# Seven block products in place of eight for 28 pairs of row tiles in the down projection

## The chip, the cores and the metric

The kernel runs on one core of one Trainium2 chip. The metric is device time in microseconds (us) of one execution; lower is better. Three runs of the kernel before gave 2377.18, 2375.62 and 2376.84 us, median 2376.84 us. A profile is one more execution, taken by the hardware profiler, with a time of its own.

Engines are named as the profile names them: PE (TensorE's matmuls), PEld (its weight loads), DVE (VectorE), ACT (ScalarE), POOL (GpSimd), SP (SyncE, which issues most of the transfers).

## The reference

Two layers, each a mixer and a gated MLP, on x of 256 rows by 2048 columns, all float32. The change concerns the last product of the MLP:

```python
def conv_ffn(h, w_gate, w_up, conv_w, conv_b, w_down):
    ...
    return (jax.nn.silu(conv) * (h @ w_up)) @ w_down

def reference(x, ...):
    for l in range(DEPTH):
        h = rms_norm(x, ln1_g[l])
        x = x + hybrid_mixer(h, w_in[l], ret_norm_g[l], q_norm_g[l], k_norm_g[l], w_out[l])
        h = rms_norm(x, ln2_g[l])
        x = x + conv_ffn(h, w_gate[l], w_up[l], conv_w[l], conv_b[l], w_down[l])
    return x
```

`w_down[l]` has 5632 rows and 2048 columns, so the product is 256 by 5632 times 5632 by 2048, added to x.

## The kernel before

The whole program is one list of **units**, written in the order in which PE is to do them. A unit is 512 KB of one weight matrix and all matmuls that use it. Four modes say what a unit holds. In `wm` it is two row tiles (128 rows each) by 512 columns; in `wm2` one row tile by 1024 columns; `ws2` and `ws4` have the weights as the stationary operand. The down projection has 44 row tiles. Each column half of 1024 columns is a chunk of 44 `wm2` units; only the second half of the last layer is two chunks of 22 `wm` units, so that the first of them can be finished and stored under the second.

Every float32 operand is held as two parts, high and low, so that a product is three matmuls (`mm3`: high by high, high by low, low by high). For weights the two parts are made on the fly: ACT copies the raw tile to `whi` (line 56), DVE subtracts that from the raw tile into `wlo` (line 57). For the activations of the down projection they are in `gT`.

A `wm2` unit is thus 12 matmuls of 128x512: two column chunks, two row halves of the output, three each. Its four sums stand in four PSUM banks for all 44 units; the pool has eight banks and hands them out in rotation.

The order on each engine is that of the program text. The last loop goes through the units, and for unit i it

- lets SP load the raw tiles up to unit i+3 (four raw buffers, tag `raw`),
- emits `prepare` up to unit i+2 (three pairs of `whi`, `wlo`),
- emits unit i's matmuls,
- emits whatever `later` and `at_unit` put into the slots of unit i: the ends of chunks, norms, transposes.

A pair of `whi`, `wlo` can be written again only when PE has left the unit that used it, so ACT and DVE follow PE three units ahead, and each engine takes its instructions strictly in the order in which they were emitted.

At the end of a chunk `x_done` calls `finalize` (lines 151 to 162): DVE adds the banks to `xs` (line 156), ACT sums squares (`junk`, line 162) or, in the last layer, the result is stored. One and two slots later `transposed` lets PE turn the new x (line 181) into two banks, ACT and DVE split that into `h` (lines 64 and 66), which the next layer's first units read. The four `h` tiles (h0 to h3) hold the normed input of whichever product comes next; in the down projection they are free until the next layer's x is turned.

The temporaries of the gate and up chunks are in a pool `ffnw`, which stays open through the down projection.

Of the kernel before, what the change touches and what calls it, by code (L numbers as in the profile page):

```python
# [10 lines left out]
F32 = mybir.dt.float32  # L11
F32R = mybir.dt.float32r
AF = mybir.ActivationFunctionType
# [3 lines left out]
P = 128  # L17
S = 256
# [15 lines left out]
def trunk(ctx, tc, x, ln1_g, w_in, ret_norm_g, q_norm_g, k_norm_g, w_out, ln2_g,  # L34
# [80 lines left out]


    units = []
    slots = {}
    pre = {}
    now = [0]  # L120

    def later(n, fn, *a):
        slots.setdefault(now[0] + n, []).append((fn, a))

    def at_unit(i, fn, *a):
        slots.setdefault(i, []).append((fn, a))

    def chunk(w, col, kts, lhs, mode, done):

        box = {}  # L130
        n = len(kts)
        step = 1 if mode == "wm2" else UK
        for u in range(0, n, step):
            units.append((w, kts[u][0], col, lhs, [k for _, k in kts[u:u + step]], mode,
                          box, u == 0, u + step >= n, done))

    hT = {}
    yT = {}
# [12 lines left out]
    def finalize(c, l, which):  # L151
        add, last = fin_acc.pop("acc", None), l == L
        cs = slice(c * NC, (c + 1) * NC)
        if add is not None:
            for t in range(2):
                dve.tensor_tensor(xs[:, t, cs], add[t], xs[:, t, cs], op=OP.add)  # L156
                if last:
                    (nc.gpsimd if c < 3 else nc.sync).dma_start(xout[:, t, cs], xs[:, t, cs])
# [57 lines left out]
    def x_done(cs, l, which):  # L216
        def fn(acc):
            for i, c in enumerate(cs):
                fin_acc["acc"] = acc[2 * i:2 * i + 2]
                finalize(c, l, which)  # L220
                if l < L:
                    later(1 + i, transposed, c, l, which)
                    if c == 3:
                        norm_tail(l, which)
        return fn
# [201 lines left out]
    def open_ffn():  # L427
        st = ExitStack()
        FFN["stack"] = st
        FFN["p"] = st.enter_context(tc.tile_pool(name="ffn", bufs=1))  # L430
        FFN["w"] = st.enter_context(tc.tile_pool(name="ffnw", bufs=2))
        gT["t"] = FFN["p"].tile([P, KF, 2, S], F32R, tag="gT", name="gT")

    def close_ffn():
        FFN.pop("stack").close()

    def ffn_gate(l, c):
        def fn(acc):
# [37 lines left out]
    def ffn_up(l, c):  # L476
# [26 lines left out]
                later(i, tile_of, i)  # L503
        return fn


    kd = [(k, k) for k in range(KD)]
    for l in range(L):
        b = len(units)
        pre[b] = pre.get(b, []) + [open_attention]  # L510
        W = w_in[l]
        U = KD // UK
        RQ, RK, RV, RG, MQ, MK, MV = (i * 1024 for i in range(7))
        for hc in range(2):
            o = hc * NC
            chunk(W, MQ + o, kd, h_of, "wm", moba_qk(l, hc, "q"))
            chunk(W, MK + o, kd, h_of, "wm", moba_qk(l, hc, "k"))
            chunk(W, MV + o, kd, h_of, "wm", v_done("mv"))
            chunk(W, RK + o, kd, h_of, "ws2", ret_qk("rk"))
# [12 lines left out]
        ky = [(k, k) for k in (*range(8, 12), *range(0, 4), *range(12, 16), *range(4, 8))]  # L532
        W = w_out[l]
        for c in (0, 2):
            chunk(W, c * NC, ky, y_of, "wm2", x_done((c, c + 1), l, 2))
        b = len(units)
        pre[b] = pre.get(b, []) + [close_attention, open_ffn]
        for c in range(FF // NC):
            chunk(w_gate[l], c * NC, kd, h_of, "ws4", ffn_gate(l, c))
            chunk(w_up[l], c * NC, kd, h_of, "ws4", ffn_up(l, c))  # L540
        kf = [(k, k) for k in range(KF)]
        chunk(w_down[l], 0, kf, g_of, "wm2", x_done((0, 1), l + 1, 1))
        if l + 1 < L:
            chunk(w_down[l], 2 * NC, kf, g_of, "wm2", x_done((2, 3), l + 1, 1))
        else:
            for c in (2, 3):
                chunk(w_down[l], c * NC, kf, g_of, "wm", x_done((c,), l + 1, 1))
        b = len(units)
        pre[b] = pre.get(b, []) + [close_ffn]

    raws, parts = {}, {}

    def load(i):
        w, k, col = units[i][:3]
        if units[i][5] == "wm2":
            raws[i] = wpool.tile([P, 2, NC], F32, tag="raw", name="wraw", bufs=4)
            nc.sync.dma_start(raws[i], w[k * P:(k + 1) * P, col:col + 2 * NC].rearrange("p (c n) -> p c n", c=2))
            return
        raws[i] = wpool.tile([P, UK, NC], F32, tag="raw", name="wraw", bufs=4)
        nc.sync.dma_start(raws[i], w[k * P:(k + UK) * P, col:col + NC].rearrange("(k p) n -> p k n", p=P))  # L560

    def prepare(i):
        hi = wpool.tile([P, UK, NC], F32R, tag="whi", name="whi")
        lo = wpool.tile([P, UK, NC], F32R, tag="wlo", name="wlo")
        split(hi, lo, raws.pop(i))
        parts[i] = hi, lo

    def multiply(i):
        _, _, _, lhs, keys, mode, box, first, last, done = units[i]
        hi, lo = parts.pop(i)  # L570
# [39 lines left out]

    def load_to(i):
        nonlocal loaded
        while loaded < min(n, i):
            load(loaded)
            loaded += 1

    load_to(1)
# [31 lines left out]
    for i in range(n):  # L649
        now[0] = i  # L650
        for fn in pre.get(i, []):
            fn()
        load_to(i + 4)
        while prepared < min(n, i + 3):
            prepare(prepared)
            prepared += 1
        multiply(i)
        for fn, a in slots.pop(i, []):
            fn(*a)
# [46 lines left out]
```

## Time and profile before

| | us |
|---|---|
| median of three runs | 2376.84 (2375.62 to 2377.18) |
| profiled execution, its own time | 2376.45 |
| its span, from first to last instruction | 2374.7 |
| down projection of layer 0, first to last matmul | 943.6 to 1191.8 |
| down projection of layer 1, first to last matmul | 2124.3 to 2370.9 |

The time of the profiled execution is 1.75 us longer than its span and 0.39 us shorter than the median. PE is the engine with most busy time; since its matmuls are pipelined, the distance from one start to the next counts, not the duration of one. A busy share of DVE is a mean over stages that use it very differently, so the down projection is to be read by itself.

### The profile page before, as it was taken

How to read it: one execution, taken by the hardware profiler on the slowest of the kernel's cores; microseconds unless marked ns; L12 is line 12 of the kernel's file. 1: busy time of each engine (PE TensorE's matmuls, PEld its weight loads, DVE VectorE, ACT ScalarE, POOL GpSimd, SP SyncE). 2: the span in 40 equal slices, each digit the busy share in tenths (PEclk: the TensorE clock that was granted, in tenths of full speed). 3: DMA queues.
4: the chain of work that ended last, by engine and by line, in shares of the span. 5: the costliest groups of instructions: out<-in, count | busy, mean ns of one | idle time of the engine just before them, and what ended most of it. 6: DMA issues, size and time to landing. Idle time of an engine off the chain costs nothing.

```text
span 2374.7 us, 32732 instructions
## 1 busy us (share of the span) xinstructions
PE 2368.8 (100%) x12629; PEld 2026.5 (85%) x12629; DVE 1438.9 (61%) x1874; ACT 1160.9 (49%) x1616; POOL 182.0 (8%) x262
## 2 busy tenths in 40 slices
PE   9999999999999999999999999999999999999999
PEld 7988988888888888888889889888888888888887
DVE  5655655576676677444456565555776776774443
ACT  5444445455555555434354444545555555553333
POOL 2001000011011011000010010000100100100000
PEclk9999999999999999999999999999999999999999
DMA  7555545556656655555565555555665555655564
GB/s 243 174 163 177 179 159 182 181 187 188 188 184 193 187 187 186 189 188 181 187 190 179 158 181 174 163 183 180 189 189 188 187 187 187 187 190 191 198 198 144
DMA packets 199868, 436.14 MB, mean 184 GB/s; under 512 B 13522, under 2 KB 14162, under 8 KB 199712
## 3 DMA queue, kind: packets, MB, share of 16 engines
q1 hardware_dynamic: 198512, 430.49, 56.8%
q0 software_dynamic: 1152, 3.55, 0.4%
q8 instruction: 98, 1.61, 0.3%
q14 instruction: 58, 0.48, 0.1%
q10 hardware_dynamic: 48, 0.02, 0.0%
HBM read 431.91 MB, written 2.10 MB: 183 GB/s over the span
## 4 chain that ended last, share of the span: by engine, by line
PE 100%; DMA 0%; SPq 0%; DVE 0%; issue 0%
PE bank L598 27%; PE bank L71 16%; PE bank L70 16%; PE bank L69 16%; PE bank L599 14%; PE bank L602 3%; PE bank L604 3%; PE bank L603 3%; PE bank L181 1%; PE bank L281 0%; PE bank L334 0%; DMA xs<-in_x_dram 0%; PE bank L420 0%; PE bank L626 0%; DVE xs L156 0%; PE bank L110 0%
## 5 line engine op out<-in xcount | busy, mean ns | idle before, releaser
L57 DVE TENSOR_TENSOR wlo<-wraw,whi 128x1024 fp32r<-128x1024 f32 x816 | 1010.4, 1239 | 761.1 <-ACT whi L56 758.6
L56 ACT ACTIVATE whi<-wraw 128x1024 fp32r<-128x1024 f32 x816 | 863.2, 1059 | 919.2 <-PE bank L71 469.5
L598 PE MATMUL bank<-h,whi 128*128 128x512 f32 x2816 | 989.6, 394 | 0.0
L599 PE MATMUL bank<-h,wlo 128*128 128x256 f32 x2816 | 796.4, 283 | 0.0
L598 PEld LDWEIGHTS bank<-h,whi 128*128 128x128 f32 x2816 | 528.9, 188 | 121.9
L599 PEld LDWEIGHTS bank<-h,wlo 128*128 128x128 f32 x2816 | 529.4, 188 | 0.1
L69 PE MATMUL bank<-whi,gT 128*128 128x512 f32 x704 | 278.4, 395 | 0.0
L70 PE MATMUL bank<-wlo,gT 128*128 128x512 f32 x704 | 278.2, 395 | 0.0
L71 PE MATMUL bank<-whi,gT 128*128 128x512 f32 x704 | 278.2, 395 | 0.0
L69 PE MATMUL bank<-whi,h 128*128 128x512 f32 x640 | 255.9, 400 | 0.0
L71 PE MATMUL bank<-whi,h 128*128 128x512 f32 x640 | 252.8, 395 | 0.0
L70 PE MATMUL bank<-wlo,h 128*128 128x512 f32 x640 | 252.7, 395 | 0.0
L464 POOL TENSOR_TENSOR sr<-cv,rb 128x256 f32<-128x256 f32 x88 | 105.1, 1194 | 870.5 <-ACT cv L463 870.5
L71 PEld LDWEIGHTS bank<-whi,gT 128*128 128x128 f32 x704 | 132.2, 188 | 32.2
L69 PEld LDWEIGHTS bank<-whi,gT 128*128 128x128 f32 x704 | 132.2, 188 | 31.9
L70 PEld LDWEIGHTS bank<-wlo,gT 128*128 128x128 f32 x704 | 132.2, 188 | 31.8
L602 PE MATMUL bank<-h,whi 128*128 128x256 f32 x512 | 145.2, 284 | 0.0
L71 PEld LDWEIGHTS bank<-whi,h 128*128 128x128 f32 x640 | 120.5, 188 | 28.5
L604 PE MATMUL bank<-h,wlo 128*128 128x256 f32 x512 | 144.4, 282 | 0.0
L603 PE MATMUL bank<-h,whi 128*128 128x256 f32 x512 | 144.1, 282 | 0.0
L70 PEld LDWEIGHTS bank<-wlo,h 128*128 128x128 f32 x640 | 120.8, 189 | 26.2
L69 PEld LDWEIGHTS bank<-whi,h 128*128 128x128 f32 x640 | 120.8, 189 | 26.0
(135 smaller groups left out, 1895.4 us busy)
## 6 DMA issues: line engine op xcount, KB each, us to landing
wraw<-in_w_in_dram SPq DMA_DIRECT2D x224, 512.0 KB, 3.7
wraw<-in_w_gate_dram SPq DMA_DIRECT2D x176, 512.0 KB, 3.9
wraw<-in_w_up_dram SPq DMA_DIRECT2D x176, 512.0 KB, 4.3
wraw<-in_w_down_dram SPq DMA_DIRECT2D x176, 512.0 KB, 3.6
wraw<-in_w_out_dram SPq DMA_DIRECT2D x64, 512.0 KB, 3.7
xs<-in_x_dram SPq DMA_DIRECT2D x3, 512.0 KB, 9.3
dec<-in_decay_dram POOLq DMA_DIRECT2D x2, 768.0 KB, 5.6
out_dram<-xs POOLq DMA_DIRECT2D x6, 256.0 KB, 4.6
```

The costliest lines, as they stand in the source:

```text
L56: act.activation(hi, src, AF.Copy)
L57: dve.tensor_tensor(lo, src, f(hi), op=OP.subtract)
L69: pe.matmul(o, a_hi, b_hi, start=first, stop=False, **kw)
L70: pe.matmul(o, a_hi, b_lo, start=False, stop=False, **kw)
L71: pe.matmul(o, a_lo, b_hi, start=False, stop=last, **kw)
L181: pe.transpose(pt[:, kk, t * P:(t + 1) * P], xs[:, t, cs + k * P:cs + (k + 1) * P], ident)
L464: pool.tensor_tensor(sr[:, i], cv, row["rb"], op=OP.mult)
L598: pe.matmul(acc[c], hi[:, j, cs], a, start=st, stop=False)
L599: pe.matmul(acc[c][:, :S], lo[:, j, cs], a[:, 0], start=False, stop=sp)
L602: pe.matmul(o, hi[:, j, cs], a[:, 0], start=st and c % 2 == 0, stop=False, skip_group_check=True)
L603: pe.matmul(o, hi[:, j, cs], a[:, 1], start=False, stop=False, skip_group_check=True)
L604: pe.matmul(o, lo[:, j, cs], a[:, 0], start=False, stop=sp, skip_group_check=True)
```

## The change

Take two row tiles of `w_down`, k and k+1, two column chunks of 512, and the two row halves of the output: a 2 by 2 block product, eight block products as written. For 14 such pairs per layer (6 in the first column half, 8 in the second, 28 in all) the kernel after makes it from seven block products of sums of blocks, in the manner of Strassen and Winograd. A pair becomes four units in place of two:

- `s1`: 6 matmuls, raw tile k+1 as it is, one of its products with an activation sum,
- `s0`: 3 matmuls, one half of raw tile k,
- `s2`: 6 matmuls, on two sums of weight blocks,
- `s3`: 6 matmuls, on raw tile k+1, whose second half now holds a sum.

The sums of weight blocks are four additions of 128x512 on DVE, in place in the raw tiles, ahead of the split of `s2` (`prepare`). The sums of activations are made by `left_side`, four times per layer (`LEFT1`, at units 6, 11, 28 and 62 of the 116 units of the two halves), each for two pairs, in five steps in the slots of five successive units: an addition of 128x1024, two and two small ones of 256 elements, ACT's copy to the high part, DVE's subtraction for the low part. They lie in the tiles h0 to h3, so the turning of chunks 0 and 1 of the next layer's x waits until the last pair of the second half is done (`next_x`).

Four of the seven products' sums need banks of their own, so a half uses all eight banks; the second half takes over the first half's banks crosswise (`box2["from"]`). After the last pair of a half, `combine_of` adds the four extra banks into x with eight DVE additions of 128x512 in three slots.

Between the units of a pair stand ordinary `wm2` units (`P`): two or three per pair. From unit 6 of the down projection to its end, two more raw tiles and a fourth pair of `whi`, `wlo` are used, in the place of the pool `ffnw`. Loads are now issued whenever a raw tile is free, and `prepare` is emitted whenever a pair is free. The second half of the last layer is made as in layer 0, so all four stores of it come at the end, on SP.

```diff
+    def left_side(k, tag, src, steps=(0, 1, 2, 3)):
+        tA = TA["t"]
+        a11, a21, a12, a22 = (tA[:, :, i] for i in range(4))
+        flat = tA.rearrange("p q a c -> p q (a c)")
...
+        def first():
+            dve.tensor_tensor(tA.rearrange("p q (k t) c -> p (q k) (t c)", k=2), f(src[:, k:k + 4, 0]),
+                              f(src[:, k:k + 4, 1]), op=OP.add)
+        def second():
+            dve.tensor_tensor(a22, a21, a22, op=OP.subtract)
+            dve.tensor_tensor(a21, a11, a21, op=OP.subtract)
+        def third():
+            dve.tensor_tensor(a11, a22, a11, op=OP.subtract)
+            dve.tensor_tensor(a12, a12, a11, op=OP.add)
+        def high():
...
+            act.activation(e[0][:, :, 0], flat, AF.Copy)
+        def low():
+            dve.tensor_tensor(e[0][:, :, 1], flat, f(e[0][:, :, 0]), op=OP.subtract)
...
+        first()
+        for n, g in zip(steps, (second, third, high, low)):
+            later(1 + n, g)
...
+    LEFT1 = ((0, 6), (1, 11), (2, 28), (3, 62))
...
+                seq = [("s1", *q), None, ("s0", *q), ("s2", *q), None, ("s3", *q)] + [None] * (g - 2)
+                o += [rest.pop(0) if x is None else x for x in seq]
+            return o + rest
+        a = order(range(0, 12, 2), range(12, KF), 11, (3, 3, 3, 3, 3, 2))
+        b = order(range(0, 16, 2), range(16, KF), 4, (2, 3, 2, 3, 2, 3, 2, 2))
...
-        chunk(w_down[l], 0, kf, g_of, "wm2", x_done((0, 1), l + 1, 1))
-        if l + 1 < L:
-            chunk(w_down[l], 2 * NC, kf, g_of, "wm2", x_done((2, 3), l + 1, 1))
-        else:
-            for c in (2, 3):
-                chunk(w_down[l], c * NC, kf, g_of, "wm", x_done((c,), l + 1, 1))
+        quads(w_down[l], 0, g_of, order1, E, box1, combine_of((0, 1), ()), x_done((0, 1), l + 1, 1))
...
+        quads(w_down[l], 2 * NC, g_of, order2, E, box2, combine_of((2, 3), (next_x,)), x_done((2, 3), l + 1, 1))
...
+        if mode == "s2":
+            r1, r2 = (raws[x][0] for x in more)
+            dve.tensor_tensor(r1[:, 1], r1[:, 1], r1[:, 0], op=OP.add)
+            dve.tensor_tensor(r1[:, 0], r2[:, 0], r1[:, 0], op=OP.add)
+            dve.tensor_tensor(r2[:, 0], r1[:, 1], r2[:, 0], op=OP.add)
+            dve.tensor_tensor(r2[:, 1], r2[:, 0], r2[:, 1], op=OP.add)
+        if mode == "s0":
+            split(hi[:, 0], lo[:, 0], raw[:, 1])
+        else:
+            split(hi, lo, raw)
...
+            s2, s3, s4, s1 = (E[k[0]][:, :, x] for x in range(4))
+            for b, c, a in {"s1": (("c", 0, s4), ("a", 1, k2[:, :, 0:P])),
+                            "s0": (("1", 0, k1[:, :, 0:P]),),
+                            "s2": (("7", 0, s3), ("5", 1, s1)),
+                            "s3": (("6", 0, s2), ("b", 1, k2[:, :, P:]))}[kind]:
+                mm3(acc[b], a[:, 0], a[:, 1], hi[:, c], lo[:, c], *ends[b])
```

Three places show how the instructions stand now. First DVE in the first half of the down projection. Before, it has nothing but splits there (`L57`), up to the adds of the chunk's end:

```order
L495 TENSOR_TENSOR gT<-u_8850,gT 128x256
L57 TENSOR_TENSOR wlo<-wraw,whi 128x1024
L495 TENSOR_TENSOR gT<-u_8873,gT 128x256
L57 TENSOR_TENSOR wlo<-wraw,whi 128x1024 x38
L156 TENSOR_TENSOR xs<-bank,xs 128x512 x4
```

Now, from the four weight sums of the first pair (`L733` to `L736`) past the second `left_side` (`L497` to `L506`):

```order
L733 TENSOR_TENSOR wraw<-wraw 128x512
L734 TENSOR_TENSOR wraw<-wraw 128x512
L735 TENSOR_TENSOR wraw<-wraw 128x512
L736 TENSOR_TENSOR wraw<-wraw 128x512
L57 TENSOR_TENSOR wlo<-wraw,whi 128x1024
L497 TENSOR_TENSOR tA<-gT 128x1024
L57 TENSOR_TENSOR wlo<-wraw,whi 128x1024
L501 TENSOR_TENSOR tA<-tA 128x2x128
L502 TENSOR_TENSOR tA<-tA 128x2x128
L57 TENSOR_TENSOR wlo<-wraw,whi 128x1024
L505 TENSOR_TENSOR tA<-tA 128x2x128
L506 TENSOR_TENSOR tA<-tA 128x2x128
```

Between two splits there now stand other DVE instructions; the second sums of activations are made while the first two pairs are multiplied. The rows that follow are two splits, the low part of those sums (`L514`), a split, the half split of `s0` and the next four weight sums.

Second, PE in the first pair (bank and tile numbers kept; `e` is a tile of activation sums). Before, a `wm2` unit's 12 matmuls go to four banks in turn; its first rows are:

```order
L69 MATMUL bank_8811<-whi_8995,gT_4020 128x512
L70 MATMUL bank_8811<-wlo_8996,gT_4020 128x512
L71 MATMUL bank_8811<-whi_8995,gT_4020 128x512
L69 MATMUL bank_8812<-whi_8995,gT_4020 128x512
L70 MATMUL bank_8812<-wlo_8996,gT_4020 128x512
```

Now the unit `s3` is six matmuls, on `whi_104`, and the next unit's follow at once:

```order
L69 MATMUL bank_8133<-whi_104,e_8045 128x512
L70 MATMUL bank_8133<-wlo_105,e_8045 128x512
L71 MATMUL bank_8133<-whi_104,e_8045 128x512
L69 MATMUL bank_7855<-whi_104,gT_3594 128x512
L70 MATMUL bank_7855<-wlo_105,gT_3594 128x512
L71 MATMUL bank_7855<-whi_104,gT_3594 128x512
L69 MATMUL bank_7856<-whi_7974,gT_3594 128x512
```

A unit with 1024 columns of weights to split lasts half as long on PE as before, and over the program PE has 84 matmuls fewer: 28 pairs by 21 in place of 24.

Third, DVE at the end of layer 0's down projection, where `h_...` are the next layer's inputs (`L66`), `L190` the adds of the last chunk. Before:

```order
L57 TENSOR_TENSOR wlo<-wraw,whi 128x1024 x42
L156 TENSOR_TENSOR xs<-bank,xs 128x512 x4
L190 TENSOR_REDUCE ms<-ssx 128x2
L191 TENSOR_SCALAR ms<-ms 128x2
L57 TENSOR_TENSOR wlo<-wraw,whi 128x1024
L66 SCALAR_TENSOR_TENSOR h_10509<-bank,par,h_10509 128x256 x4
```

Now:

```order
L526 TENSOR_TENSOR xs<-xs,tA 128x512 x2
L66 SCALAR_TENSOR_TENSOR h_9323<-bank,par,h_9323 128x256 x4
L57 TENSOR_TENSOR wlo<-wraw,whi 128x1024
L190 TENSOR_TENSOR xs<-bank,xs 128x512 x4
L224 TENSOR_REDUCE ms<-ssx 128x2
L225 TENSOR_SCALAR ms<-ms 128x2
L66 SCALAR_TENSOR_TENSOR h_9370<-bank,par,h_9370 128x256 x4
```

The split of the first `h` chunk has moved from the middle of the down projection to its last unit but one, ahead of the last weight split and of the adds that empty the four banks.

## Rows read from the trace of the kernel before

**Rows 1.** Page, part 1: busy us (share of span), instructions

```profile
PE 2368.8 (100%) x12629; PEld 2026.5 (85%) x12629; DVE 1438.9 (61%) x1874; ACT 1160.9 (49%) x1616; POOL 182.0 (8%) x262
```

**Rows 2.** Page, part 4: the chain of waits by engine

```profile
PE 100%; DMA 0%; SPq 0%; DVE 0%; issue 0%
```

**Rows 3.** Down projections: length, busy us (x) of PE, PEld, DVE, ACT, POOL; PEclk, DMA, GB/s

```profile
943.60:1190.00 246.40, 246.40 (x1067) 198.30 (x1066) 116.43 (x111) 100.73 (x111) 0.00 (x0) 1.00 0.54 186
2123.00:2374.00 251.00, 247.89 (x1065) 199.50 (x1063) 115.59 (x107) 93.84 (x94) 3.35 (x6) 1.00 0.54 184
```

**Rows 4.** Timeline in `w_down`: start, us, what [idle before <-releaser]

```profile
999.61 0.39 PE L69 MATMUL bank<-whi,gT 128*128 128x512 f32 x1
999.81 1.06 ACT L56 ACTIVATE whi<-wraw 128x1024 fp32r<-128x1024 f32 x1 [1.74 <-PE bank L71]
...
1000.90 1.23 DVE L57 TENSOR_TENSOR wlo<-wraw,whi 128x1024 fp32r<-128x1024 f32 x1 [1.57 <-ACT whi L56]
...
1002.61 1.06 ACT L56 ACTIVATE whi<-wraw 128x1024 fp32r<-128x1024 f32 x1 [1.74 <-PE bank L71]
```

**Rows 5.** Timeline of DVE in a gate chunk, where it runs back to back

```profile
563.91 0.42 DVE L452 TENSOR_TENSOR u<-bank,u 128x256 f32<-128x256 f32 x1
564.36 0.43 DVE L453 TENSOR_TENSOR a<-u,rb 128x256 f32<-128x256 f32 x1
...
570.95 0.42 DVE L453 TENSOR_TENSOR a<-u,rb 128x256 f32<-128x256 f32 x1
571.29 1.22 DVE L57 TENSOR_TENSOR wlo<-wraw,whi 128x1024 fp32r<-128x1024 f32 x1
```

**Rows 6.** DVE groups by shape: busy us, mean ns of one, idle before

```profile
L57 DVE TENSOR_TENSOR wlo<-wraw,whi 128x1024 fp32r<-128x1024 f32 x816 | 1010.4, 1239 | 761.1 <-ACT whi L56 758.6
...
L453 DVE TENSOR_TENSOR a<-u,rb 128x256 f32<-128x256 f32 x88 | 37.6, 427 | 3.0
...
L156 DVE TENSOR_TENSOR xs<-bank,xs 128x512 f32<-128x512 f32 x32 | 20.0, 683 | 5.4 <-PE bank L71 5.4
...
L270 DVE TENSOR_TENSOR raw<-raw,fac 128x512 f32<-128x512 f32 x8 | 5.9, 738 | 0.3
```

**Rows 7.** Page, part 6: transfers of `w_down`, KB each, us to landing

```profile
wraw<-in_w_down_dram SPq DMA_DIRECT2D x176, 512.0 KB, 3.6
```

**Rows 8.** Timeline of DVE, then PE, then ACT where layer 0 ends

```profile
1190.25 1.23 DVE L57 TENSOR_TENSOR wlo<-wraw,whi 128x1024 fp32r<-128x1024 f32 x1 [1.57 <-ACT whi L56]
1191.39 2.48 DVE L156 TENSOR_TENSOR xs<-bank,xs 128x512 f32<-128x512 f32 x4
...
1194.55 1.03 PE L181 MATMUL bank<-ident,xs 128*128 128x128 f32 x8
1195.34 0.48 PE L69 MATMUL bank<-whi,h 128*128 128x512 f32 x1
...
1195.96 1.55 ACT L64 ACTIVATE h<-bank,par 128x256 fp32r<-128x256 f32 x4
```

**Rows 9.** Timeline of the last 5 us: DVE, then SP's queue

```profile
2370.93 0.69 DVE L156 TENSOR_TENSOR xs<-bank,xs 128x512 f32<-128x512 f32 x1 [0.71 <-PE bank L71]
...
2370.25 1.75 SPq L158 DMA_DIRECT2D out_dram<-xs  x2
```

**Rows 10.** Timeline of PE in the first 11 us

```profile
6.88 1.11 PE L181 MATMUL bank<-ident,xs 128*128 128x128 f32 x4 [0.53 <-DMA xs<-in_x_dram]
...
9.07 0.63 PE L70 MATMUL bank<-wlo,h 128*128 128x512 f32 x1
9.50 0.63 PE L71 MATMUL bank<-whi,h 128*128 128x512 f32 x1
...
10.53 0.39 PE L71 MATMUL bank<-whi,h 128*128 128x512 f32 x1
10.76 0.40 PE L69 MATMUL bank<-whi,h 128*128 128x512 f32 x1
```

More of the change, by code (lines that the diff above doesn't have):

```diff
@@ L117, in trunk @@
     units = []
+    loads = []
     slots = {}
@@ L133, in chunk, with quads, adds @@
         for u in range(0, n, step):
-            units.append((w, kts[u][0], col, lhs, [k for _, k in kts[u:u + step]], mode,
+            loads.append((w, kts[u][0], col, mode))
+            units.append((len(loads) - 1, (), lhs, [k for _, k in kts[u:u + step]], mode,
                           box, u == 0, u + step >= n, done))
+    def quads(w, col, lhs, order, extra, box, combine, done):
+        total = {}
+        def adds(kind):
+            return {"P": "abcd", "s1": "ac", "s0": "1", "s2": "57", "s3": "b6"}[kind]
+        flat = []
+        at = {}
+        for it in order:
+            if isinstance(it, int):
+                loads.append((w, it, col, "wm2"))
+                flat.append(("P", it, len(loads) - 1, ()))
+                continue
+            kind, k1, k2 = it
+            if kind == "s1":
+                loads.append((w, k2, col, "wm2"))
+                loads.append((w, k1, col, "wm2"))
+                at[k1] = len(loads) - 1
+            flat.append((kind, (k1, k2), at[k1] - (1 if kind in ("s1", "s3") else 0),
+                         (at[k1], at[k1] - 1) if kind == "s2" else ()))
+        for i, (kind, *_) in enumerate(flat):
+            for b in adds(kind):
+                total.setdefault(b, []).append(i)
+        last_s = max((i for i, x in enumerate(flat) if x[0] != "P"), default=-1)
+        for i, (kind, k, ld, more) in enumerate(flat):
+            ends = {b: (total[b][0] == i, total[b][-1] == i) for b in adds(kind)}
+            units.append((ld, more, lhs, k, kind, box, ends, i == len(flat) - 1, done))
+            if i == last_s:
+                at_unit(len(units) - 1, combine, box)
     hT = {}
@@ L221, in fn @@
                 if l < L:
[L222 removed]
+                    if c > 1 or which == 2:
+                        later(1 + i, transposed, c, l, which)
                     if c == 3:
@@ L434, in close_ffn, with open_down @@
     def close_ffn():
+        FFN.pop("dstack").close()
         FFN.pop("stack").close()
+    E, TA = {}, {}
+    def open_down(end):
+        FFN.pop("wstack").close()
+        st = ExitStack()
+        FFN["dstack"] = st
+        p = st.enter_context(tc.tile_pool(name="down", bufs=1))
+        TA["t"] = p.tile([P, 2, 4, P], F32, tag="tA", name="tA")
+        for i in range(2):
+            rfree.append((p.tile([P, 2, NC], F32, tag=f"rawx{i}", name="wraw"), end))
+        wfree.append((p.tile([P, UK, NC], F32R, tag="hix", name="whi"),
+                      p.tile([P, UK, NC], F32R, tag="lox", name="wlo"), end))
@@ new lines, in combine_of, with add, fn, one @@
+    def combine_of(pair, bs):
+        lo_, hi_ = (slice(c * NC, (c + 1) * NC) for c in pair)
+        def add(t, cs, x, op=OP.add):
+            dve.tensor_tensor(xs[:, t, cs], xs[:, t, cs], x, op=op)
+        def fn(box):
+            p1, p5, p6, p7 = (box["acc"][b] for b in "1567")
+            v, w = (TA["t"][:, i].rearrange("p a c -> p (a c)") for i in range(2))
+            act.activation(v, p1, AF.Copy)
+            def one():
+                add(0, hi_, p1)
+                dve.tensor_tensor(v, p6, v, op=OP.add)
+                add(0, lo_, p5)
+            def two():
+                dve.tensor_tensor(w, p7, v, op=OP.add)
+                add(1, lo_, p5)
+                add(0, lo_, v, OP.subtract)
+            def three():
+                add(1, hi_, w)
+                add(1, lo_, w, OP.subtract)
+                for g in bs:
+                    g()
+            later(1, one)
+            later(2, two)
+            later(3, three)
+        return fn
@@ L504, in ffn_up, with down_orders, order @@
         return fn
+    LEFT1 = ((0, 6), (1, 11), (2, 28), (3, 62))
+    def down_orders():
+        def order(pairs, rest, first, gaps):
+            rest = list(rest)
+            o = [rest.pop(0) for _ in range(first)]
+            for k, g in zip(pairs, gaps):
+                q = (k, k + 1)
+                seq = [("s1", *q), None, ("s0", *q), ("s2", *q), None, ("s3", *q)] + [None] * (g - 2)
[3 more added lines that the diff above has]
+        b = order(range(0, 16, 2), range(16, KF), 4, (2, 3, 2, 3, 2, 3, 2, 2))
+        return a, b
     kd = [(k, k) for k in range(KD)]
@@ L541, in trunk, with left, next_x @@
         kf = [(k, k) for k in range(KF)]
[L542 to L547 removed]
+        b = len(units)
+        order1, order2 = down_orders()
+        end = b + len(order1) + len(order2)
+        pre[b + 6] = [lambda end=end: open_down(end)]
+        def left(j):
+            left_side(4 * j, f"h{j}", gT["t"])
+        for j, i in LEFT1:
+            at_unit(b + i, left, j)
+        box1, box2 = {}, {}
+        box2["from"] = box1
+        quads(w_down[l], 0, g_of, order1, E, box1, combine_of((0, 1), ()), x_done((0, 1), l + 1, 1))
+        def next_x(l=l):
+            if l + 1 < L:
+                later(1, transposed, 0, l + 1, 1)
+                later(2, transposed, 1, l + 1, 1)
+        quads(w_down[l], 2 * NC, g_of, order2, E, box2, combine_of((2, 3), (next_x,)), x_done((2, 3), l + 1, 1))
         b = len(units)
@@ L562, in prepare @@
[L562 to L570, printed above, removed]
+    rfree = [(wpool.tile([P, UK, NC], F32, tag=f"raw{i}", name="wraw", bufs=1), 1 << 30) for i in range(4)]
+    wfree = [(wpool.tile([P, UK, NC], F32R, tag=f"whi{i}", name="whi", bufs=1),
+              wpool.tile([P, UK, NC], F32R, tag=f"wlo{i}", name="wlo", bufs=1), 1 << 30) for i in range(3)]
@@ new lines, in trunk, with take @@
+    user, final = {}, {}
+    for i, u in enumerate(units):
+        for ld in (u[0], *u[1]):
+            user.setdefault(ld, i)
+            final[ld] = i
+    def take(free, i):
+        for at, x in enumerate(free):
+            if i < x[-1]:
+                return free.pop(at)
+    def load(i):
+        w, k, col, mode = loads[i]
+        got = take(rfree, final[i])
+        if got is None:
+            return False
+        raws[i] = got
+        if mode == "wm2":
+            nc.sync.dma_start(got[0], w[k * P:(k + 1) * P, col:col + 2 * NC].rearrange("p (c n) -> p c n", c=2))
+        else:
+            nc.sync.dma_start(got[0], w[k * P:(k + UK) * P, col:col + NC].rearrange("(k p) n -> p k n", p=P))
+        return True
@@ new lines, in prepare @@
+    def prepare(i):
+        ld, more, mode = units[i][0], units[i][1], units[i][4]
+        got = take(wfree, i)
+        if got is None:
+            return False
+        hi, lo = got[:2]
+        raw = raws[ld][0]
+        if mode == "s2":
[6 more added lines that the diff above has]
+            split(hi[:, 0], lo[:, 0], raw[:, 1])
+        else:
+            split(hi, lo, raw)
+        for x in {ld, *more}:
+            if final[x] == i:
+                rfree.append(raws.pop(x))
+        parts[i] = got
+        return True
@@ new lines, in seven @@
+    def seven(i):
+        _, _, lhs, k, kind, box, ends, last, done = units[i]
+        hi, lo = parts[i][:2]
+        acc = box.setdefault("acc", {})
+        other = box.get("from")
+        for b, like in zip("abcd1567", "1567abcd"):
+            if b in ends and ends[b][0]:
+                acc[b] = other["acc"][like] if other else bank()
+        if kind == "P":
+            a = lhs(k)
+            for b, c, t in (("c", 0, 0), ("d", 0, 1), ("a", 1, 0), ("b", 1, 1)):
+                ts = slice(t * P, (t + 1) * P)
+                mm3(acc[b], a[:, 0, ts], a[:, 1, ts], hi[:, c], lo[:, c], *ends[b])
+        else:
+            k1, k2 = lhs(k[0]), lhs(k[1])
+            s2, s3, s4, s1 = (E[k[0]][:, :, x] for x in range(4))
[4 more added lines that the diff above has]
+                mm3(acc[b], a[:, 0], a[:, 1], hi[:, c], lo[:, c], *ends[b])
+        wfree.append(parts.pop(i))
+        if last:
+            done([acc[b] for b in "cdab"])
@@ L571, in multiply @@
+    def multiply(i):
+        if units[i][4][0] in "Ps":
+            seven(i)
+            return
+        _, _, lhs, keys, mode, box, first, last, done = units[i]
+        hi, lo = parts[i][:2]
+        wfree.append(parts.pop(i))
         if first:
@@ L612, in load_to @@
         nonlocal loaded
-        while loaded < min(n, i):
-            load(loaded)
+        while loaded < min(len(loads), i) and load(loaded):
             loaded += 1
@@ L652, in trunk @@
             fn()
-        load_to(i + 4)
-        while prepared < min(n, i + 3):
-            prepare(prepared)
+        load_to(len(loads))
+        while prepared < n and max((units[prepared][0], *units[prepared][1])) < loaded and prepare(prepared):
             prepared += 1
+            load_to(len(loads))
         multiply(i)
```

15 lines of the change are left out of this document (8 added, 7 removed).

## The prediction, made before the changed kernel ran

> **What bounds the kernel now.** First the page's busy shares: PE fills the span, DVE 61% of it [rows 1]. A busy PE could still be waiting inside pipelined matmuls, so next the chain of waits: all of it is PE, none DVE or DMA [rows 2]. Then the stages the change touches. In both down projections PE has no gap up to the last 4 us, and DVE is busy 116 of 246 us, 47%, POOL not at all in layer 0 [rows 3]. The timeline there shows the beat [rows 4]: ACT's copies start 2.80 us apart (999.81, 1002.61), once per unit of 12 matmuls, so a matmul costs PE 2.80/12 = 0.2333 us. ACT starts 0.20 after PE's next unit has begun, since the high part it overwrites is free only then; DVE starts 0.03 after ACT ends and then idles 1.57 us. So time is PE's matmul count times 0.2333, as long as the splits keep ahead of it. The change takes matmuls from PE and gives DVE work; the question is whether DVE still keeps ahead, pair by pair and not on the mean.
>
> **What goes.** 28 pairs by 24 - 21 = 3 matmuls: 84 by 0.2333 = 19.6 us.
>
> **DVE's prices.** A full split holds DVE 1.14 us from start to next start (1190.25 to 1191.39 [rows 8]), its result is there after 1.23. An instruction that needs the one before it starts 0.03 after that one's end (563.91 + 0.42 to 564.36), one that doesn't 0.08 before it (570.95 + 0.42 to 571.29 [rows 5]). An addition of 128x512 all in SBUF is not in the trace of a split. Between 427 ns for 256 elements and 1239 for 1024, 512 come to 0.69; the addition with one operand in a bank takes 683 ns [rows 6]. The four weight sums depend on one another, so I take 0.72 each, 2.88 together. From below: four additions in a row that need nothing of each other take 2.48, about 0.61 each [rows 8]. From above: 738 ns, the slowest form of that size [rows 6], plus 0.03.
>
> [...]
>
> **A pair on DVE.** Weight sums 2.88. ACT can copy the sums only after the last of them, and DVE waits for that copy: 0.03 + 1.06 + 0.03 = 1.12, and no other work stands between. The half split 0.69 + 0.03, three full splits 3.42. Together 8.14, and 1.14 per ordinary unit beside it. PE needs 21 by 0.2333 = 4.90 for the pair and 2.80 per ordinary unit. With three ordinary units: DVE 11.56, PE 13.30, 1.7 to spare. With two: 10.42 against 10.50, nothing to spare.
>
> **The activations' sums** cost DVE 1.14, then two by (0.45 + 0.34) [rows 5], then 1.14 for the low part: 3.9 us, four times a layer. The first set is made among ordinary units ahead of all pairs, with 1.57 us idle per unit to lie in. The other three lie among pairs, and there the steps, each one small, add up between one `s2` and the next:
>
> - Second set, in pairs 1 and 2. Pair 1's `s2` comes just in time: from PE leaving unit 9, ACT's half copy (about 0.6, between 0.39 for 256 elements [rows 8] and 1.06 for 1024 [rows 4]), the half split, the first set's low part, the sums, the wait and the split take about 8.0, while PE has 7.7 of work and needs the low part 0.23 later. From there to the next `s2`: 11.56 + 3.9, and 1.0 because ACT's copy of the activation sums waits for DVE and stands ahead of the next unit's copy in ACT's queue. 16.4 against 13.30: PE waits 3.1.
> - Third set, at unit 28: 11.56 + 2.72 (all but the low part) is 14.3 against 13.30. A pair with three ordinary units leaves a margin of about 0.5 to 0.9, since the half split can't start before PE has left the unit four earlier; I take 0.5. Wait 0.5, and then the low part stands between the splits of `s2` and of the next unit: 1.17 + 1.14 on DVE while PE spends 1.40 on `s2`, 0.9 more. 1.4.
> - Fourth set, at unit 62, beside a pair with two ordinary units: 10.42 + 2.72 - 10.50 - 0.5 = 2.1, and the same 0.9: 3.0.
> - Three pairs that follow a pair with two ordinary units: the half split waits for a unit that PE leaves 1.40 before the pair; from there 0.20 + 0.6 + 0.03 + 0.72 + 2.88 + 1.12 + 1.23 = 6.8, so the split is there 5.4 into the pair, and PE wants it at 4.90 + 0.23. 0.3 each, 0.8.
>
> 8.3 a layer, 16.6 in both. Behind a waiting PE stands only more PE; ACT and DVE gain nothing from its pause, because they are what it waits for.
>
> **The end of layer 0.** The turning of chunk 0 of the next x, its four `h` copies on ACT and its splits on DVE now stand ahead of the last unit's weight split and the adds that empty the banks; and with all eight banks in use, the next layer's first two sums get two of those banks. From PE leaving the last unit but one: PE itself has 0.79 (eight turns), 2.80, 0.79, so 4.4. DVE has emptied the third bank after half the turns 0.4, the `h` copies 1.5, ACT's weight copy 1.06, the split 1.14, three adds 1.9, with handovers 6.1 [rows 8]. PE waits 1.7. Before, the banks were others and nothing waited. If DVE's queue were empty there, it would be 0; if the copies came wholly after the turns, 2.2.
>
> **The end of the program.** All four last stores of 256 KB are issued on SP within the last 2.1 us of matmuls, not two. The last add still starts 0.2 after PE's end, and stores landed about 3 us later [rows 9]. Two transfers more ahead of the last one: 0 to 1.4, I take 0.4.
>
> **Edits at nothing.** `combine`'s eight additions, 5 us, lie under four or five ordinary units with 1.6 idle each; without that cover they would cost up to 5 a half. The loads: a raw tile lands 3.6 us after issue [rows 7]; a pair holds two of the six tiles, four are left, so each load is out more than one unit's 2.80 ahead. The new loop emits loads earlier but SP still waits for the same readers. Turned chunks 0 and 1: the same PE work, moved.
>
> **Sum.** -19.6 + 16.6 + 1.7 + 0.4 = -0.9, on the profiled execution's 2376.45: 2375.5. The median stands 0.4 above it: 2375.9. With weight sums at 0.61 a pair loses 0.44 less: the three larger waits shrink by 0.4 each, the three small ones go, 6.3 a layer, 2371.9. With 0.77, and 0.09 for each restart of PE (a first matmul after other work shows 0.48 in place of 0.39 [rows 4, 8]), 10.5 a layer, 2380.3.
>
> **Rivals.**
>
> - *DVE hides it.* DVE would have some 116 + 14 by 4.7 for the pairs + 4 by 4.2 for the activations' sums + 16 by 0.69 for `combine`, 210 us of work in 246 a layer, 85%, so on the mean there is room, and the fourth buffer pair lets it run ahead. If nothing waited but the layer's end: 2376.8 - 19.6 + 1.7 + 0.4 = 2359; with a third of the waits gone, 2370. Against it: the wait for ACT within each pair is not DVE work and can't be moved, and the waits are worked out between neighbouring `s2`, where a mean doesn't help. 0.25.
> - *PE loses its clock in the pauses (slower).* [...] 0.10.
> - *The hand-over costs more than 0.03.* Every pair has four chains PE to ACT to DVE to PE in place of two, and DVE to ACT besides; with 0.1 per hand-over the small waits grow to about 0.6 in all eight pairs with two ordinary units or after them, and a raw tile that comes late would do the same: 5 to 8 more, 2381 to 2384. For: DVE to PE is nowhere a wait in the trace, so its delay isn't shown. 0.10.
> - That the matmuls don't go is excluded: the order has 84 fewer.
>
> **How the numbers follow.** My forecast, between 2371.9 and 2380.3, has 0.55. Faster than 2372.1 (0.2%, about what a measurement of this kernel can tell) is the first rival and a little of my lower end: 0.28. Slower than 2381.6 are the second and most of the third: 0.17. Within: 0.55. The range leaves out the far end of the first rival and of the last two: 2368 to 2383.
>
> **What would show it.** PE: 84 matmuls fewer, and idle time of 7 to 10 us in each down projection, released by DVE's split, in waits of 2 to 3 us around units 15 to 21 and 62 to 70, small ones at `s2` elsewhere; about 1.7 at the next layer's first matmul, released by the adds. DVE: the sums at 0.66 to 0.72, and about 1.1 idle ahead of each `s2` split, released by ACT's copy. Wrong it would be if PE's waits sum to less than 12 or more than 24, if matmuls after a wait start 0.43 apart, or if PE waits for a transfer.

## The result, and the profile after

The changed kernel takes 2358.95 us, the median of 4 runs (2358.75 to 2359.33), where the kernel before took 2376.49 beside it (4 runs, 2375.62 to 2377.18). The ratio is 0.9927, 95% interval 0.9909 to 0.9944: faster by 17.5 us, and outside the range that I gave. A second measurement of the same kernel gave 0.9926 (0.9914 to 0.9939; run e7 below). What came out is the first rival, "DVE hides it", at its 2359.

The page of the kernel after, parts 1 and 4, answers to [rows 1, 2]: 84 matmuls fewer, DVE 167 us busier, and DVE in the chain of waits with 1%.

```profile
PE 2346.7 (100%) x12545; PEld 2008.4 (85%) x12545; DVE 1605.7 (68%) x2122; ACT 1210.1 (51%) x1684; POOL 180.8 (8%) x260
...
PE 98%; DVE 1%; issue 0%; ACT 0%; DMA 0%; ACTq 0%
```

The two down projections, cut at their first and last matmul (length, busy us of PE, PEld, DVE, ACT, POOL, then granted clock, DMA share and GB/s). Of the kernel before, which [rows 3] cut a little differently:

```profile
943.60:1191.70 248.10, 248.10 (x1074) 199.67 (x1073) 117.88 (x113) 100.94 (x111) 0.00 (x0) 1.00 0.54 187
2124.30:2370.70 246.40, 246.40 (x1058) 198.37 (x1056) 113.93 (x105) 93.45 (x93) 3.35 (x6) 1.00 0.54 184
```

Of the kernel after:

```profile
942.92:1181.30 238.38, 237.06 (x1024) 190.87 (x1023) 198.66 (x232) 124.30 (x141) 0.00 (x0) 1.00 0.57 194
2114.79:2352.30 237.51, 236.20 (x1016) 189.91 (x1014) 197.27 (x229) 118.13 (x127) 2.26 (x4) 1.00 0.56 189
```

Layer 1 is the clean one: 42 matmuls fewer, 8.9 us shorter. In layer 0 another 8 matmuls (0.8 us) are turns that now stand behind the last matmul of the product and are not saved; without them it is 8.9 as well. DVE is busy 83% of the stage (197.27 of 237.51), as the first rival had worked out (85%), and PE has 1.3 us of idle time in each. By the distances between the starts of matmuls, as far as they exceed 0.2333, the waits cost 2.1 us a layer, since a matmul after a wait also holds PE 0.1 longer. I had forecast 8.3.

**Where the 8.3 went.** DVE in one pair of the kernel after (start, length, what it does, and the idle time before it with its releaser):

```profile
970.89 0.69 DVE L57 TENSOR_TENSOR wlo<-wraw,whi 128x512 fp32r<-128x512 f32 x1 [0.24 <-ACT whi L56]
...
972.63 0.69 DVE L733 TENSOR_TENSOR wraw<-wraw 128x512 f32<-128x512 f32 x1
973.36 0.69 DVE L734 TENSOR_TENSOR wraw<-wraw 128x512 f32<-128x512 f32 x1
974.08 0.69 DVE L735 TENSOR_TENSOR wraw<-wraw 128x512 f32<-128x512 f32 x1
974.81 0.69 DVE L736 TENSOR_TENSOR wraw<-wraw 128x512 f32<-128x512 f32 x1
975.41 1.22 DVE L57 TENSOR_TENSOR wlo<-wraw,whi 128x1024 fp32r<-128x1024 f32 x1
```

And ACT in the same pair:

```profile
974.16 2.20 ACT L56 ACTIVATE whi<-wraw 128x1024 fp32r<-128x1024 f32 x2 [3.31 <-DVE wraw L734]
```

ACT's copy for `s2` starts 0.11 after the end of the second sum (L734, at 974.05), not after the fourth, and runs while DVE makes the third and the fourth. So DVE goes from the last sum to the split with no idle time, here and in 26 of the 28 pairs. (In the first pair of each second half it idles 0.90 there, because it is ahead: the copy waits for PE to leave its buffers.) The code says why: `s2` splits the first raw tile alone, and the first two sums complete that tile; the last two write the two halves of the second tile, and of those sums only `s3` makes use. The 1.12 us of waiting that I put into each pair aren't there.

**What waits are left.** PE around unit 69, where the fourth set of activation sums meets a pair:

```profile
1088.11 0.40 PE L69 MATMUL bank<-whi,e 128*128 128x512 f32 x1
1089.20 0.50 PE L70 MATMUL bank<-wlo,e 128*128 128x512 f32 x1 [0.70 <-DVE wlo L57]
1089.54 0.39 PE L71 MATMUL bank<-whi,e 128*128 128x512 f32 x1
...
1090.47 0.39 PE L69 MATMUL bank<-whi,gT 128*128 128x512 f32 x1
1091.47 0.50 PE L70 MATMUL bank<-wlo,gT 128*128 128x512 f32 x1 [0.62 <-DVE wlo L57]
```

By the distances between starts, as above, the first wait costs 0.86 and the second 0.77, each with 0.11 more at the matmul behind it. Both are released by DVE's split. A third of 0.27 stands at unit 36. Nothing waits at units 15 to 21, and not at the other `s2`. Around unit 69 DVE runs without a gap, with the low part of the activations' sums between two weight splits:

```profile
1087.93 1.22 DVE L57 TENSOR_TENSOR wlo<-wraw,whi 128x1024 fp32r<-128x1024 f32 x1
1089.06 1.22 DVE L514 TENSOR_TENSOR e<-tA,e 128x1024 fp32r<-128x1024 f32 x1
1090.20 3.49 DVE L57 TENSOR_TENSOR wlo<-wraw,whi 128x1024 fp32r<-128x1024 f32 x3
```

**The end of layer 0**, DVE, then PE, answering to [rows 8]: the next layer's first matmul starts 0.14 after the adds have begun, so it waited for none of the four banks that these adds empty.

```profile
1180.86 1.23 DVE L57 TENSOR_TENSOR wlo<-wraw,whi 128x1024 fp32r<-128x1024 f32 x1
1182.00 2.48 DVE L190 TENSOR_TENSOR xs<-bank,xs 128x512 f32<-128x512 f32 x4
...
1181.35 1.03 PE L215 MATMUL bank<-ident,xs 128*128 128x128 f32 x8
1182.14 0.47 PE L69 MATMUL bank<-whi,h 128*128 128x512 f32 x1
```

**The last microseconds**, answering to [rows 9]: from the last matmul's start to the end of the span it is 5.1 us (2352.10 to 2357.2), where before it was 4.2 (2370.50 to 2374.7). Four stores stand behind one another on SP in place of two. That is not all of it: e3 below has the same four stores on SP, and 4.6 us there; the other 0.5 shows only in kernels with pairs (5.0 to 5.1 in each), and why, no run shows.

```profile
2351.15 2.44 SPq L192 DMA_DIRECT2D out_dram<-xs  x4
2352.10 0.40 PE L71 MATMUL bank<-whi,gT 128*128 128x512 f32 x1
```

**The sum as it came.** 84 by 0.2333 saved, 19.6; waits 4.2 in place of 0; the tail 0.9; matmuls that start closer together, 2.4 less (run e3 below); the first down projection begins 0.7 earlier (it begins at 942.7 to 943.8 in the profiles of the seven runs below, 943.6 before, so this is not shown to be the change's doing). -19.6 + 4.2 + 0.9 - 2.4 - 0.7 = -17.6; the spans differ by 17.5 (2374.7 to 2357.2).

### The profile page after: what moved, and what is told of

Read it like the earlier page. It is cut to its first block, busy times and chain, and to the rows that moved or that the text cites. A ratio compares the mean times of both kernels' runs of the same rounds, so it can differ in the third digit from the quotient of the medians.

```text
span 2357.2 us, 32926 instructions
## 1 busy us (share of the span) xinstructions
PE 2346.7 (100%) x12545; PEld 2008.4 (85%) x12545; DVE 1605.7 (68%) x2122; ACT 1210.1 (51%) x1684; POOL 180.8 (8%) x260
## 4 chain that ended last, share of the span: by engine, by line
PE 98%; DVE 1%; issue 0%; ACT 0%; DMA 0%; ACTq 0%
PE bank L806 28%; PE bank L70 16%; PE bank L71 16%; PE bank L69 16%; PE bank L807 14%; PE bank L810 3%; PE bank L812 3%; PE bank L811 3%; PE bank L215 1%; DVE wlo L57 1%; PE bank L316 0%; PE bank L369 0%; PE bank L455 0%; ACT whi L56 0%; DMA stage<-in_ln_g_dram 0%
## 5 line engine op out<-in xcount | busy, mean ns | idle before, releaser
L57 DVE TENSOR_TENSOR wlo<-wraw,whi 128x1024 fp32r<-128x1024 f32 x872 | 1054.8, 1220 | 570.2 <-ACT whi L56 567.5
L56 ACT ACTIVATE whi<-wraw 128x1024 fp32r<-128x1024 f32 x872 | 903.3, 1045 | 830.7 <-PE bank L71 296.0
L70 PE MATMUL bank<-wlo,gT 128*128 128x512 f32 x564 | 222.7, 395 | 1.2 <-DVE wlo L57 1.2
L69 PE MATMUL bank<-whi,gT 128*128 128x512 f32 x564 | 222.5, 394 | 0.0
L71 PE MATMUL bank<-whi,gT 128*128 128x512 f32 x564 | 222.0, 394 | 0.0
L70 PEld LDWEIGHTS bank<-wlo,gT 128*128 128x128 f32 x564 | 105.9, 188 | 27.7 <-DVE wlo L57 3.0
L69 PEld LDWEIGHTS bank<-whi,gT 128*128 128x128 f32 x564 | 105.9, 188 | 25.0
L71 PEld LDWEIGHTS bank<-whi,gT 128*128 128x128 f32 x564 | 105.9, 188 | 25.1
```

Of the source, the lines that this page charges most:

```text
L56: act.activation(hi, src, AF.Copy)
L57: dve.tensor_tensor(lo, src, f(hi), op=OP.subtract)
L69: pe.matmul(o, a_hi, b_hi, start=first, stop=False, **kw)
L70: pe.matmul(o, a_hi, b_lo, start=False, stop=False, **kw)
L71: pe.matmul(o, a_lo, b_hi, start=False, stop=last, **kw)
```

## The experiments

All seven were compared with the kernel before on their chip, which measured 2375.87 us (19 runs, e1 to e4) and 2376.2 (10 runs, e5 to e7).

**e1: the wait that I had predicted, put in.** ACT reads one column of the last sum ahead of its copy for `s2`:

```diff
             dve.tensor_tensor(r2[:, 1], r2[:, 0], r2[:, 1], op=OP.add)
+            act.activation(probe, r2[:, 1, NC - 1:NC], AF.Copy)
```

> Changed kernel with one thing added: ACT reads one column of the last of the four weight sums before it copies the tile of s2, so that the copy waits for all four additions as the prediction had it, and not for the second. Theory (the prediction failed in that one step: the copy runs beside the third and fourth addition, so the 1.12 us of DVE idle per pair do not exist): with the wait made real DVE idles 1.1 to 1.4 us ahead of each of the 28 splits of s2, and PE's waits rise from 2.1 us a layer to 7 to 10; time 2359 + 10 to 16 = 2369 to 2375. Rival (DVE's lead of four units absorbs a wait of that size wherever it comes from): PE's waits stay under 4 a layer, time 2359 to 2363.

Measured: 2372.18 us (10 runs, 2371.04 to 2374.68), ratio 0.9985 (0.9975 to 0.9994). One such wait in each of 28 pairs takes back 13 to 14 of the 17.5 us (12 by the stages of the two profiles: 6.8 in layer 0, 5.2 in layer 1). DVE now idles 1.22 ahead of each of the 28 splits, here in the same pair as above:

```profile
974.93 0.69 DVE L737 TENSOR_TENSOR wraw<-wraw 128x512 f32<-128x512 f32 x1
976.84 1.23 DVE L57 TENSOR_TENSOR wlo<-wraw,whi 128x1024 fp32r<-128x1024 f32 x1 [1.22 <-ACT whi L56]
```

PE's waits are 7.3 us in layer 1, at the places of my prediction: second set 2.4 (forecast 3.1), third 1.6 (1.4), fourth 3.2 (3.0), the small ones none (0.8). So the working from `s2` to `s2` was sound in the main, and what it was given was wrong. In layer 0 PE's losses are 8.9, because of something else:

```profile
991.85 0.40 PE L71 MATMUL bank<-whi,gT 128*128 128x512 f32 x1
993.38 0.51 PE L69 MATMUL bank<-whi,e 128*128 128x512 f32 x1 [1.13 <-ACT whi L56]
994.64 0.50 PE L70 MATMUL bank<-wlo,e 128*128 128x512 f32 x1 [0.76 <-DVE wlo L57]
994.98 0.55 PE L71 MATMUL bank<-whi,e 128*128 128x512 f32 x1
995.33 0.63 PE L69 MATMUL bank<-whi,e 128*128 128x512 f32 x1
995.75 0.63 PE L70 MATMUL bank<-wlo,e 128*128 128x512 f32 x1
```

After two waits of 1.30 and 1.03 with one matmul between them, matmuls start 0.43 apart, as at 9.07 and 9.50 in [rows 10] (where the profile gives the granted clock as 1.00, so those matmuls are read from their distances alone). Here the granted clock (third figure from the end) falls to 0.51:

```profile
995.00:997.00 2.00, 2.00 (x6) 1.56 (x5) 2.00 (x3) 1.32 (x3) 0.00 (x0) 0.51 0.59 188
997.00:999.00 2.00, 2.00 (x7) 1.59 (x6) 2.00 (x2) 0.90 (x1) 0.00 (x0) 0.63 0.89 266
999.00:1005.00 6.00, 6.00 (x28) 4.83 (x27) 3.52 (x6) 1.58 (x2) 0.00 (x0) 1.00 0.71 270
```

That costs 1.5 us. In layer 1 the same two waits (1.31 and 1.03) weren't followed by it.

**e2: DVE freed of the sums.** The four weight sums of each pair are left out, so the raw tiles are multiplied as they are.

```diff
         if mode == "s2":
-            r1, r2 = (raws[x][0] for x in more)
-            dve.tensor_tensor(r1[:, 1], r1[:, 1], r1[:, 0], op=OP.add)
...
+            pass
```

> Changed kernel without the four weight sums of each pair (28 by 4 additions of 128x512 left out; s2 and s3 then split the raw tiles). Theory: what PE still waits (2.1 us a layer, at units 36, 69 and 70) is DVE's load between two s2; with 2.9 us a pair gone it vanishes: 2359 - 4 = 2355, no wait of PE on DVE in w_down. Rival (the waits belong to the activations' sums alone, whose low part stands between two splits): the one at unit 70 stays, about 0.8 a layer, 2357.

Measured: 2355.44 us (4 runs), ratio 0.9916 (0.9901 to 0.9931), 3.5 below the kernel after. PE's waits fall from 2.1 to 0.43 a layer, 3.3 in both, so all that 112 sums still cost is what PE waits for in two or three places. The theory holds but for one wait that is left, at unit 70, where the low part alone stands ahead of the split:

```profile
1089.54 0.50 PE L70 MATMUL bank<-wlo,gT 128*128 128x512 f32 x1 [0.17 <-DVE wlo L57]
```

**e3: everything but the pairs.** All units are ordinary ones again, in the new loop and with the fourth pair of parts; no activation sums. The next layer's x is turned behind its own chunk again, and the second half takes banks of its own (both left out of the excerpt).

```diff
-        a = order(range(0, 12, 2), range(12, KF), 11, (3, 3, 3, 3, 3, 2))
-        b = order(range(0, 16, 2), range(16, KF), 4, (2, 3, 2, 3, 2, 3, 2, 2))
-        return a, b
+        return list(range(KF)), list(range(KF))
...
-        for j, i in LEFT1:
-            at_unit(b + i, left, j)
```

> Changed kernel with all 44 row tiles as ordinary units, no activation sums, no combine: all 84 matmuls are back, but the new loop, the fourth pair of parts and the two more raw tiles from unit 6 of w_down stay. Theory (PE's matmul count is what counts, and the starts of matmuls stand a little closer on units that use the fourth pair, 0.230 against 0.233 us, because of where it lies): time before less 2 to 3 us plus up to 1 at the end, 2374 to 2376, and the distance of matmuls by pair is the same as in the changed kernel. Rivals: the gain lies in buffers and loop, not in the matmuls: 2360 to 2368; or the distance belongs to the pairs' units: every matmul 0.2333 and 2377.

Measured: 2374.53 us (10 runs), ratio 0.9994 (0.9984 to 1.0004): with the interval, no change. The rest of the edit is worth at most a microsecond or two. But its two down projections, with the same counts of PE's instructions as before the change, are each 1.2 us shorter from the first matmul's start to the last one's (246.74 and 244.97, before 247.92 and 246.17):

```profile
942.77:1189.60 246.83, 246.83 (x1074) 199.34 (x1073) 117.69 (x113) 100.78 (x111) 0.00 (x0) 1.00 0.55 188
2122.30:2367.40 245.10, 245.10 (x1058) 197.59 (x1056) 113.84 (x105) 93.16 (x93) 2.26 (x4) 1.00 0.53 183
```

Neither has a pause of PE, so the matmuls start closer: 1.2 us over some 1060 is 0.0011 each. The two stages together are the term of -2.4 above. Matmuls on the fourth pair's tiles (every fourth unit, from unit 9 on) start 0.2283 apart in the mean here, on the three others 0.2333, as before the change. In the kernel after, ordinary units show the same two values to 0.0005 (0.2288 and 0.2332), and the units of the pairs 0.232 in the mean, without a clear difference by tile. In e4, which has no fourth pair of parts, ordinary units start 0.2332 apart and the pairs' units 0.232. So the larger part goes with the fourth pair's tiles, and in the kernel after a smaller part with the pairs' units; why, and whether it is because of where those tiles lie, no run shows.

**e4: without the fourth pair of parts.**

```diff
-        wfree.append((p.tile([P, UK, NC], F32R, tag="hix", name="whi"),
-                      p.tile([P, UK, NC], F32R, tag="lox", name="wlo"), end))
```

> Changed kernel without the fourth pair of whi and wlo in w_down (the two more raw tiles stay), so splits can run three units ahead of PE and not four. Theory (the lead is what lets DVE carry a pair's work past its short units): PE waits ahead of nearly every s2, 0.4 to 1.6 us, up to 3 at the fourth activation sum, some 12 to 17 us a layer; 2359 + 20 to 30 = 2379 to 2389, slower than before. Rival (DVE has room on the mean, 83% busy, three pairs do): under 2364.

Measured: 2385.57 us (4 runs, 2383.35 to 2385.72), ratio 1.0039 (1.0024 to 1.0054): slower than before the change, with the same 84 matmuls gone. The losses by the distances between starts are 14.2 us a layer, in some twenty places. DVE can't begin a split before PE has left the unit three earlier, so it can't use its free time among ordinary units to run ahead. And both layers show the fall of the clock (0.57 in the mean from 2284.0 to 2287.6), here of layer 1, PE:

```profile
2279.93 0.39 PE L71 MATMUL bank<-whi,gT 128*128 128x512 f32 x1
2281.63 0.49 PE L69 MATMUL bank<-whi,e 128*128 128x512 f32 x1 [1.31 <-ACT whi L56]
2283.05 0.50 PE L70 MATMUL bank<-wlo,e 128*128 128x512 f32 x1 [0.93 <-DVE wlo L57]
...
2283.94 0.63 PE L70 MATMUL bank<-wlo,e 128*128 128x512 f32 x1
2284.37 0.63 PE L71 MATMUL bank<-whi,e 128*128 128x512 f32 x1
```

Waits of 1.47 and 1.19, then ten matmuls in 3.88 us where 2.33 were due: 1.55, in each layer.

**e5: the activations' sums at one unit** in place of small steps over four:

```diff
-    def left_side(k, tag, src, steps=(0, 1, 2, 3)):
+    def left_side(k, tag, src, steps=(0, 0, 0, 0)):
```

> Changed kernel with the activations' sums made at once: the four later steps (two and two small additions, ACT's copy, the low part) all in the slot one unit after the first, not in four successive ones. Theory (DVE stands through ACT's copy, 1.1 us, and the whole 2.7 us lie between two splits): PE waits 1 to 2 us at each of the three sets that lie among pairs, 5 to 6 us a layer in place of 2.1: 2359 + 5 to 9 = 2364 to 2368. Rival (the lead of four units hides that too): 2359 to 2361.

Measured: 2368.73 us (5 runs), ratio 0.9967 (0.9954 to 0.998), 0.7 over the upper end that I expected. It is 10 us slower than the kernel after, and PE's waits are 6.6 a layer in place of 2.1 (9.0 in both). PE's waits in layer 0's down projection, by cause (us, times, longest):

```profile
PE bank L70 <- DVE wlo L57: 4.1, 5, 0.9
PE bank L69 <- ACT whi L56: 0.8, 1, 0.8
```

Among the pairs, DVE has the steps behind the first one in one piece of 4.1 us between two splits (979.66 to 983.72), 1.1 of it idle:

```profile
981.03 0.42 DVE L506 TENSOR_TENSOR tA<-tA 128x256 f32<-128x256 f32 x1
982.58 1.23 DVE L514 TENSOR_TENSOR e<-tA,e 128x1024 fp32r<-128x1024 f32 x1 [1.12 <-ACT e L511]
```

So the small steps are worth as much as half of the gain: DVE has the room, but not 4.1 us of it in one piece. Part of that piece is a wait for ACT's copy of the kind that I had wrongly put into each pair: here nothing stands between the sums and the subtraction that needs the copy. What the wait and what the length of the piece cost, each by itself, no run shows.

**e6: the fourth set eight units later**, so that its first steps lie between the `s2` of units 69 and 76, beside a pair with three ordinary units and not with two:

```diff
-    LEFT1 = ((0, 6), (1, 11), (2, 28), (3, 62))
+    LEFT1 = ((0, 6), (1, 11), (2, 28), (3, 70))
```

> Changed kernel with the fourth set of activation sums begun at unit 70 and not at unit 62 (it is needed from unit 99 on): its first and small steps then lie between the s2 of units 69 and 76, a pair with three ordinary units. Theory (the two waits of 0.86 and 0.77 us at units 69 and 70 come from it alone): they go and only the 0.2 at unit 36 stays, 3.5 us less, 2355 to 2356. Rival (the load is moved, not removed: the same 10.0 against 10.5 us holds at every pair with two ordinary units): 1 to 2 us of waits at units 76 or 82 instead, 2358 to 2360.

Measured: 2355.22 us (4 runs), ratio 0.9912 (0.9898 to 0.9925). It beats both kernels, the one after by 3.55 on the same chip. One wait of 0.27 a layer is left, at unit 36; at units 76 and 82, where the rival had the load move to, there is none:

```profile
1019.56 0.40 PE L69 MATMUL bank<-whi,gT 128*128 128x512 f32 x1
1019.96 0.50 PE L70 MATMUL bank<-wlo,gT 128*128 128x512 f32 x1
```

2.1 less 0.27 is 1.8 a layer, 3.7 in both: the waits and nothing else. PE then has next to no pause in either down projection.

**e7: the kernel after again**, beside e5 and e6.

> The changed kernel itself, for the comparison on this chip: 2359, PE's waits 2.1 us a layer at units 36, 69 and 70.

Measured: 2358.77 us (5 runs, 2358.73 to 2359.33), ratio 0.9926 (0.9914 to 0.9939).

## Why the prediction was wrong

- *What goes*, 84 matmuls by 0.2333: right.
- *DVE's prices*: right. The groups by shape of the kernel after (busy us, mean ns of one, idle before) give the sums 692 ns where I took 690, and the half split 686:

```profile
L736 DVE TENSOR_TENSOR wraw<-wraw 128x512 f32<-128x512 f32 x28 | 19.4, 692 | 1.0
...
L57 DVE TENSOR_TENSOR wlo<-wraw,whi 128x512 fp32r<-128x512 f32 x28 | 19.2, 686 | 0.5 <-ACT whi L56 0.5
```

  They start 0.72 to 0.73 apart in a chain (972.63, 973.36, 974.08, 974.81), where I took 0.72.
- *A pair on DVE*: this is the step that failed. "ACT can copy the sums only after the last of them, and DVE waits for that copy ... 1.12, and no other work stands between." ACT's copy hangs on the second of the four sums, and the other two are the work that stands between. A pair costs DVE 6.9 (1084.42, its half split, to 1087.93, the split of `s2`, 3.5, and three splits by 1.13), not 8.14. I read the sums as one chain with one result; which tile each one writes, and which tile the copy reads, stood in the function's lines. I then used the same wait as the reason against the rival: "can't be moved". e1 puts the wait in and gets 7.3 of the 8.3 forecast, and its time of 2372.18 lies in my range, at the lower end.
- *The activations' sums*: the fourth set was right in kind, first at `s2`, then at the low part between two splits (1.9 in place of 3.0; less 1.12 that is 1.9). The third left 0.27 of 1.4. The second left none of 3.1: 0.9 by the same working without the two waits of 1.12, and e1 shows that I had this place 0.7 too dear. The three small ones, 0.8, aren't there even in e1.
- *The end of layer 0*, 1.7: nothing, a second term that was wrong. I had the next layer's sums wait for banks that the last adds empty; they started while these ran. Which banks they got, the trace doesn't tell.
- *The end of the program*: 0.9 in place of 0.4, inside its bounds of 0 to 1.4; e3, with the four stores on SP and no pairs, shows the 0.4.
- *What I cost at nothing*: `combine`, the loads and the new loop stayed hidden: PE has no wait in the slots of `combine` or for a load, and e3, in the new loop, has none at all in the two stages. What I didn't foresee is the closer matmuls, 2.4.
- *The rivals*: "DVE hides it" was right in its main point, DVE's room and the lead of four units, and got 0.25; the chance hung on one reading of one operand. That its 2359 came out to the microsecond is partly luck: it added 2.1 for the ends of the layer and of the program, where the runs show 4.2 of waits and 0.9 at the end, less 2.4 and 0.7 that it didn't have, 2.0. "PE loses its clock in the pauses": e1 and e4 show such falls, to 0.51 (e1, 995 to 997), each at 1.5 to 1.55 us, but in the changed kernel none shows: its longest wait is 0.86, and around unit 69 the granted clock stays at 1.00. A single pause over 2 us stands in no down projection of these runs (the longest distance between two starts is 1.70, in e4); the falls came behind two waits with one matmul between them, and not each time. No run shows what makes up 2383, the far end of this rival: the profile of e1 has one fall, that of e4 two, 3.1 us together. "The hand-over costs more": DVE to ACT does take 0.11 (974.05 to 974.16), DVE to PE 0.05 (1089.15 to 1089.20), yet the small waits that this was to lengthen aren't there, not even in e1.

## What to carry to other kernels

When one engine makes several results in a row and another copies one of them, look up which instruction writes the last piece that the copy reads: the rest of the row is cover for the copy, and the row's length is not a wait. When an engine has room on the mean, look at how far it may run ahead (buffers) and how long its longest uninterrupted piece is: here one more pair of buffers was worth 27 us (3 of them the two falls of the clock in e4) and cutting the additions into steps 10, where the whole gain is 17.5. And extra work that fell between tightly packed pieces cost 3.55 us even at 83% load (the kernel after against e6); eight units later, beside a pair with one ordinary unit more, it was free.

## What the runs showed of the hardware

- The granted clock fell to 0.51 (e1, 995 to 997 us) after short pauses. Two waits, with one matmul between them, of 2.66 us together were followed by a fall in both layers (e4), of 2.33 in one layer and not in the other (e1), of 2.2 in neither (e1 at the fourth set, e5). Each fall cost 1.5 us (e1) to 1.55 (e4). PE waited there for ACT's copy and DVE's split, among matmuls that otherwise run without a gap. What sets off a fall, no run shows.
- The distance between matmul starts differs a little with the tile that PE reads: 0.228 on the fourth pair's tiles in ordinary units, 0.2333 on the others (e3). Over two stages the closer starts make 2.4 us, 0.1% of the time and not clear of noise in e3's interval, but plain in the trace. Why stays open.
- PE's first matmul after a wait holds it 0.33 to 0.34 rather than 0.23 (1089.20 to 1089.54 in the kernel after), so a wait costs about 0.1 beyond its idle time.
